# A two-layer hybrid transformer block on one core: elementwise steps moved off GpSimd, and modulation rows made in a layout of 128 channels a partition

## The chip, the core and the metric

The kernel runs on one core of one Trainium2 chip. The metric is the device time of one execution in microseconds. The core has five engines with instruction queues of their own: TensorE (PE in the profile; its weight loads PEld), VectorE (DVE), ScalarE (ACT), GpSimd (POOL) and SyncE (SP), which here issues nearly all DMAs. Each engine takes its instructions in the order written for it.

## What is computed

Two layers over 256 context and 256 latent tokens of 1024 channels. In each, three mixers run on projections of the modulated input (neighbourhood attention, RWKV-7, mLSTM); their outputs go through `w_out`, a residual sum and a layer norm, and then through a routed mixture of 32 experts (two per token) with a residual sum and a second norm. Cut to the lines that the change touches:

```python
for l in range(DEPTH):                                   # 2
    sh1, sc1, g1, sh2, sc2, g2 = split(silu(c) @ w_mod[l] + b_mod[l], 6)   # one row of 1024 each; other rows for ctx
    ...
    y_ctx, y_lat = token_mixers(p_ctx, p_lat, na_rpb[l], ...)
    x = layer_norm(alpha * x + g1 * dot(y_lat, w_out[l]), ln1_g[l], ln1_b[l])
    h2 = x * (1 + sc2) + sh2                             # the same for ctx in layer 0
    f = hierarchical_moe(h2, ...)
    x = layer_norm(alpha * x + g2 * f, ln2_g[l], ln2_b[l])

def neighbourhood_attention(...):    # s_loc = q.k * scale + bias from rpb, inside a window
def _rwkv_output(...):               # (head_norm(y) * ln_w + ln_b + bonus) * gate
```

All arithmetic is in f32 or its TensorE form (`fp32r`). In layer 1 only the latent tokens go past the mixers.

## The kernel before

Tokens lie on the 128 partitions in four tiles (0 and 1 context, 2 and 3 latents); layer 1 uses two of them behind the mixers. A layer runs through these stages, with the times of layer 0 / layer 1: projections and mixers (0 to 420 / 1085 to 1440 us), out stage (420 to 533 / 1440 to 1506), routing (533 to 548 / 1506 to 1520), expert blocks (548 to 1085 / 1520 to 2000), second norm.

A scheduler orders each engine's instructions from priorities and gives tiles their buffers. Work of one stage fills gaps of another: the projections of the attention and the mLSTM (`ps<-rg,wh` in the trace) lie between the steps of the RWKV inversion, and the `w_out` products (`pw<-rg,q`, `rg,yrw`, `rg,O`) between the attention's. In `moe` the order is the one that is written, and an expert weight ring of 1 MB pieces streams from DRAM once the routing has written the expert table.

The steps that the change touches:
- The RWKV chunk inversion (L754 and L756 on VectorE, 64 x n x n, growing n) and the T updates (L769), whose results TensorE takes up through ScalarE's copy L824. T then feeds the product PV x MA (`pw<-PV,MA`) and the ones behind it.
- `na_bias1` loads a bias table of 128 x 2048 (16 DMAs of 64 KB from `rpb`) and adds the window's mask to it, L1238 on GpSimd. There are two a layer. Attention takes them up much later.
- `headnorm` (L890) and `rwkv_out` (L906): mean, square (L899), variance, scale; transposes; sum with the bonus (L923).
- `out_rows` (L1378), called for tile 0 and tile 2: three modulation rows are broadcast from the DRAM tile `modd` to 128 partitions (512 KB each on the SBUF side), and four GpSimd instructions fold the first norm's scale and shift into them (L1383 to L1387).
- `out_item` (L1389), one a token tile: `w_out` product in two halves, residual (L1406, L1407), statistics (L1339, L1341), the routed input h (L1415, L1416, with the rows of `out_rows`), its transposes and logits, its split into an upper part `hi` (L1440, ScalarE) and a lower part `lo` (L1441, GpSimd), and the norm of the residual stream z, whose scale and shift are L1444 and L1445 on GpSimd.
- L1901, on GpSimd, scales the g2 rows by 1/ALPHA.

Of the kernel before, what the change touches and what calls it, by code (L numbers as in the profile page):

```python
# [9 lines left out]
F32 = mybir.dt.float32  # L10
# [4 lines left out]
AF = mybir.ActivationFunctionType  # L15
ALU = mybir.AluOpType
# [3 lines left out]
D = 1024  # L20
DEPTH = 2
# [5 lines left out]
ALPHA = (2.0 * DEPTH) ** 0.25  # L27
# [186 lines left out]
class K:  # L214
    def __init__(self, tc, ctx, a, dbg=None, upto=99):
        self.tc, self.nc, self.ctx, self.a = tc, tc.nc, ctx, a
        self.dbg = dbg or (lambda *x: None)
        self.upto = upto
        nc = self.nc
        self.cp = ctx.enter_context(tc.tile_pool(name="cp", bufs=1))  # L220
        self.ring = ctx.enter_context(tc.tile_pool(name="ring", bufs=NR))
        self.psp = ctx.enter_context(tc.tile_pool(name="psp", bufs=PB, space=PSUM))
        self.psw = ctx.enter_context(tc.tile_pool(name="psw", bufs=PC, space=PSUM))
        self.pse = ctx.enter_context(tc.tile_pool(name="pse", bufs=PE_, space=PSUM))
        if CFG["PD"]:
            self.psd = ctx.enter_context(tc.tile_pool(name="psd", bufs=CFG["PD"], space=PSUM))
        self.n = 0
        self.pin = False
        cp = self.cp
        self.cst = cp.tile([P, _CN], F32, name="cst")  # L230
        self.prm = cp.tile([P, DEPTH, _NP], F32, name="prm")
        self.ident = self.c("ident")
        self.one = cp.tile([P, 1], F32, name="one")
        nc.vector.memset(self.one, 1.0)
        self.epsc = cp.tile([P, 4], F32, name="epsc")
        for i, e in enumerate((LN_EPS, RW_EPS, ML_EPS, LN_EPS / ALPHA ** 2)):
            nc.vector.memset(self.epsc[:, i:i + 1], e)
        nc.scalar.preload_act_table_set("natural_log_exp_and_others")
        self.hp = ctx.enter_context(tc.tile_pool(name="hp", bufs=NH))
        self.wp = ctx.enter_context(tc.tile_pool(name="wp", bufs=NW))  # L240
        self.qp = ctx.enter_context(tc.tile_pool(name="qp", bufs=NQ))
        self.mp = ctx.enter_context(tc.tile_pool(name="mp", bufs=2))
        dp = ctx.enter_context(tc.tile_pool(name="dp", bufs=1, space=bass.MemoryType.DRAM))
        self.modd = [dp.tile([2, 6 * D], F32, name=f"modd{l}") for l in range(DEPTH)]
        self.xd = dp.tile([4 * P, D], F32, name="xd")
        self.nMd = dp.tile([8, 512], F32, name="nMd")
        self.eMd = dp.tile([8, 512], F32, name="eMd")
        self.dA, self.dX, self.dXT = ([dp.tile([16 * 4160], F32, name=f"{n}{i}") for i in range(4)] for n in ("dA", "dX", "dXT"))
        self.rst = cp.tile([P, 512], BF, name="rst")
        nc.gpsimd.memset(self.rst, 1.0)  # L250
        nc.gpsimd.memset(self.rst.rearrange("p (c s) -> p c s", s=64)[:, :, 0:1], 0.0)
# [638 lines left out]
    def headnorm(self, Y, n, eps, sq, s):  # L890

        nc = self.nc
        b = lambda t: t.unsqueeze(2).to_broadcast([P, n, 64])
        m = self.sm([16], s + "m", bufs=1)[:, :n]
        nc.vector.tensor_reduce(m, Y, AX.X, ALU.add)
        nc.vector.tensor_scalar(m, m, 1.0 / 64, None, ALU.mult)
        nc.vector.tensor_tensor(Y, Y, b(m), ALU.subtract)
        sq = sq[:, :n * 64].rearrange("p (n s) -> p n s", s=64)
        nc.gpsimd.tensor_tensor(sq, Y, Y, ALU.mult)  # L899
        v = self.sm([16], s + "v", bufs=1)[:, :n]  # L900
        nc.vector.tensor_reduce(v, sq, AX.X, ALU.add)
        nc.scalar.activation(v, v, AF.Ln, scale=1.0 / 64, bias=self.epsc[:, eps:eps + 1])
        nc.scalar.activation(v, v, AF.Exp, scale=-0.5)
        nc.vector.tensor_tensor(Y, Y, b(v), ALU.mult)

    def rwkv_out(self, last):  # L906
        nc = self.nc
        c0 = 4 if last else 0
        lo = c0 * 64
        self.headnorm(self.Ys[:, c0 * 128:].rearrange("p (n s) -> p n s", s=64), (8 - c0) * 2, 1, self.w("sq"), "rw")  # L910
        ys = self.Ys.rearrange("p (c x s) -> p c x s", x=2, s=64)
        self.yrw = self.w("yrw")
        for hh in range(2):
            pt = self.pw()
            for c in range(c0, 8):
                self.tr(pt[:, c * 64:(c + 1) * 64], ys[64 * hh:64 * hh + 64, c, :, :], 64 * hh)
            for ct in range(2):
                nc.scalar.activation(self.yrw[64 * hh:64 * hh + 64, ct * 512 + lo:(ct + 1) * 512], pt[64 * ct:64 * ct + 64, lo:], AF.Copy)
        for ct in range(2):
            sl = slice(ct * 512 + lo, (ct + 1) * 512)  # L920
            yo = self.yrw[:, sl]
            nc.vector.tensor_scalar(yo, yo, self.pr[:, 30 + ct:31 + ct], self.pr[:, 32 + ct:33 + ct], ALU.mult, ALU.add)
            nc.gpsimd.tensor_tensor(yo, yo, self.Vf[:, sl], ALU.add)  # L923
            pg = self.pw()
            self.mm(pg[:, lo:], self.g2w[0:64, ct * 128:(ct + 1) * 128], self.GD[0:64, lo:])
            nc.vector.tensor_tensor(yo, yo, pg[:, lo:], ALU.mult)
# [301 lines left out]
    def na_bias1(self, l, i):  # L1228

        nc = self.nc  # L1230
        rp = self.a["rpb"]
        b = self.rg((2048,))
        bv = b.rearrange("p (h r c) -> p h r c", h=8, r=4)
        for h in range(8):
            for a_ in range(2):
                off = ((l * 8 + h) * 15 + 7 - (2 * i + a_)) * 127
                nc.sync.dma_start(bv[64 * a_:64 * a_ + 64, h], bass.AP(tensor=rp.tensor, offset=off, ap=[[1, 64], [127, 4], [1, 64]]))
        nc.gpsimd.tensor_tensor(b.rearrange("p (n c) -> p n c", c=64), b.rearrange("p (n c) -> p n c", c=64),  # L1238
                                self.c("nam")[:, None, :].to_broadcast([P, 32, 64]), ALU.add)
        return b  # L1240

# [116 lines left out]
    def out_prep(self, l, last):  # L1358
        nc, a = self.nc, self.a
# [12 lines left out]
        nc.gpsimd.dma_start(self.rw, a["rtw"][l].rearrange("p (k n) -> p k n", k=KT))  # L1372
        self.rb = self.mp.tile([P, 40], F32, name=self.nm("rb"), tag="rb", bufs=1)
        nc.gpsimd.dma_start(self.rb, bass.AP(tensor=a["rtb"].tensor, offset=l * 40, ap=[[0, P], [1, 40]]))
        self.lnr = self.row(a["ln1_g"][l]), self.row(a["ln1_b"][l])
        self.Lg = self.mp.tile([P, 4, 40], F32, name=self.nm("Lg"), tag="Lg", bufs=1)

    def out_rows(self, l, i):  # L1378

        G = self.nc.gpsimd  # L1380
        lng, lnb = self.lnr
        g1, sh2, sc2 = self.rows3 = [self.row(self.modd[l][i, (2 + k) * D:(3 + k) * D]) for k in range(3)]
        G.tensor_scalar(sc2, sc2, 1.0, None, ALU.add)  # L1383
        tm = self.w("tm")
        G.tensor_tensor(tm, lnb, sc2, ALU.mult)
        G.tensor_tensor(sh2, sh2, tm, ALU.add)
        G.tensor_tensor(sc2, sc2, lng, ALU.mult)  # L1387

    def out_item(self, l, last, t):  # L1389

        nc, a = self.nc, self.a
        V, G = nc.vector, nc.gpsimd
        if t in (0, 2):
            self.out_rows(l, 1 - t // 2)
        g1, sh2, sc2 = self.rows3
        lng, lnb = self.lnr
        n = self.tl.index(t)
        z = self.acc[t]
        for hf in range(2):
            sl = slice(hf * 512, (hf + 1) * 512)  # L1400
            ps = self.pw()
            for k, kt in enumerate((4, 5, 6, 7, 0, 1, 2, 3)):
                yt, o = self.yn[kt]
                i = self.mm(ps, yt[:, o + t * 128:o + (t + 1) * 128], self.wo[kt // 2][:, kt % 2, sl], k == 0, k == 7)
            tm = self.q("tm")
# [5 lines left out]
        h2 = self.w("h2")  # L1411
        mean, rstd, nmr = self.stats(z, 0)
        for hf in range(2):
            sl = slice(hf * 512, (hf + 1) * 512)
# [17 lines left out]
        hi, lo = self.w("hi", F32R), self.w("lo", F32R)  # L1432
        self.hh_[t], self.hl_[t] = hi, lo
        pj = lambda x: x.rearrange("t (p j) -> t p j", j=KT)
# [3 lines left out]
                nc.scalar.activation(jp(hi), pj(h2), AF.Copy)  # L1438
        else:
            nc.scalar.activation(jp(hi), pj(h2), AF.Copy)  # L1440
        G.tensor_tensor(jp(lo), pj(h2), jp(hi), ALU.subtract)  # L1441
        if fin:
            self.norm_z(z, mean, rstd, nmr)
        G.tensor_tensor(z, z, lng, ALU.mult)  # L1444
        G.tensor_tensor(z, z, lnb, ALU.add)  # L1445

    def row(self, src):

# [274 lines left out]
    def moe(self, l):  # L1723
        nc = self.nc
# [50 lines left out]
        with self.tc.issue_after(self.slotted.ins):  # L1775
            for _ in self.more:
                pass
        nxt, gath = prep(*plan[1])
        run(up[4:], gath)
        for k in range(1, len(plan) + 1):  # L1780
# [73 lines left out]
    def run(self):  # L1854
# [15 lines left out]
        for l in range(DEPTH):  # L1870
# [26 lines left out]
            if self.upto == 10 * l + 2:  # L1897
                return
            for i in ((0,) if last else (1, 0)):
                self.g2b[i] = self.row(self.modd[l][i, 5 * D:6 * D])  # L1900
                nc.gpsimd.tensor_scalar(self.g2b[i], self.g2b[i], 1.0 / ALPHA, None, ALU.mult)  # L1901
            more = iter(())
            if l + 1 < DEPTH:
                more = self.mod_first(l + 1)
# [115 lines left out]
```

## Time and profile before

| | us |
|---|---|
| median of three runs | 2030.6 (2022.24 to 2033.0) |
| the profiled execution | 2033.04 |
| its span | 2031.2 |
| TensorE busy | 1800.4 (89%) |
| VectorE busy | 958.3 (47%) |
| ScalarE busy | 508.8 (25%) |
| GpSimd busy | 273.5 (13%) |

The profile is of one execution. An instruction's row gives its start, its duration, the engine, the line, the operation and the tiles. A bracket at its end tells how long the engine stood idle before it, and what released it. Wait rows sum such idle times. The granted clock is a share of TensorE's full speed: 1.00 is 2.4 GHz, 0.50 is 1.2 GHz.

### The profile page before, as it was taken

To read this page: it belongs to the slowest core of one execution; us is meant where nothing else is said; L and a number is where in the kernel's file an instruction comes from. 1 tells how busy PE (TensorE), PEld (TensorE's weight loads), DVE (VectorE), ACT (ScalarE), POOL (GpSimd) and SP (SyncE) were. 2 spreads that over 40 slices of the span, in tenths; PEclk is the share of its full clock that TensorE was granted. 3 is DMA by queue.
4 is the path that set the end of the run, shared out by engine and by line. 5 is a ranking of instruction groups with operands and counts; after the bars stand their busy time and mean duration, and the time that the engine had idled before them with its cause. 6 is when DMAs were issued, how large, how long until landed. Compare 5 with 4: busy or idle time off the path is not lost. (4 is left out here: it accounts for less than half of the span.)

```text
span 2031.2 us, 29550 instructions
## 1 busy us (share of the span) xinstructions
PE 1800.4 (89%) x11375; PEld 912.1 (45%) x11375; DVE 958.3 (47%) x2133; ACT 508.8 (25%) x1073; POOL 273.5 (13%) x204
## 2 busy tenths in 40 slices
PE   6999999799998899889996899997999988988884
PEld 2777875245533233324434677773453222323221
DVE  2686655567633334334446687744762222222223
ACT  1663413444110010001014654314521010100001
POOL 0000010034311112111221010010220001001001
PEclk9988999999999999999998899988899999999997
DMA  8432335733779998999992233347748979999995
GB/s 282 141 82 58 89 62 217 244 145 104 285 284 382 409 384 327 407 394 396 386 413 87 88 89 95 67 114 251 290 177 350 388 288 415 417 416 409 417 418 227
DMA packets 194224, 532.93 MB, mean 262 GB/s; under 512 B 77824, under 2 KB 108448, under 8 KB 156576
## 3 DMA queue, kind: packets, MB, share of 16 engines
q1 hardware_dynamic: 191936, 526.33, 68.9%
q0 software_dynamic: 992, 2.53, 0.4%
q8 instruction: 92, 1.51, 0.3%
q10 hardware_dynamic: 1152, 2.13, 0.3%
q14 instruction: 52, 0.43, 0.1%
HBM read 523.44 MB, written 7.50 MB: 261 GB/s over the span
## 5 line engine op out<-in xcount | busy, mean ns | idle before, releaser
L283 PE MATMUL ps<-rg,xe 128*32 128x512 f32 (+2 forms) x2280 | 478.0, 614 | 47.3 <-DMA rg<-in_exp_w_up_dram 27.7
L283 PE MATMUL pe<-rg,HT 128*32 128x512 f32 (+2 forms) x1120 | 236.0, 658 | 55.5 <-DMA rg<-in_exp_w_down_dram 44.4
L283 PE MATMUL ps<-rg,wh 128*128 128x512 f32 (+2 forms) x1056 | 260.0, 390 | 5.0 <-ACT wh L473 2.7
L283 PEld LDWEIGHTS ps<-rg,xe 128*32 128x32 f32 (+2 forms) x2280 | 107.8, 123 | 282.6 <-issue 180.3
L1686 DVE TENSOR_TENSOR sc<-pw,bc 128x512 f32<-128x512 f32 x164 | 112.1, 690 | 220.3 <-PE pw L283 218.9
L283 PEld LDWEIGHTS ps<-rg,wh 128*128 128x128 f32 (+1 forms) x1056 | 182.4, 195 | 53.8 <-issue 13.3
L1687 POOL TENSOR_TENSOR acc<-acc,sc 128x512 f32<-128x512 f32 x82 | 106.0, 1293 | 587.5 <-DVE sc L1686 587.5
L283 PEld LDWEIGHTS pe<-rg,HT 128*32 128x32 f32 (+2 forms) x1120 | 66.0, 131 | 220.6 <-issue 122.0
L1676 DVE SCALAR_TENSOR_TENSOR yl<-pe,sw,yh 128x512 fp32r<-128x512 f32 x54 | 40.4, 750 | 237.4 <-ACT yh L1675 234.6
L1675 ACT ACTIVATE yh<-pe,sw 128x512 fp32r<-128x512 f32 x54 | 36.9, 687 | 311.1 <-PE pe L283 288.2
L1652 ACT ACTIVATE H<-ps 128x512 f32<-128x512 f32 x27 | 16.1, 598 | 313.1 <-DVE acc L1687 302.9
L283 PE MATMUL pw<-oh,hi 128*128 128x256 f32 x336 | 90.7, 306 | 1.5 <-DVE oh L1590 1.5
L283 PE MATMUL pw<-yh,ot 128*128 128x512 f32 x164 | 84.2, 513 | 1.8 <-DVE sc L1686 1.5
L283 PE MATMUL pw<-oh,lo 128*128 128x256 f32 x336 | 83.8, 285 | 0.0
L283 PEld LDWEIGHTS pw<-yh,ot 128*128 128x128 f32 x164 | 30.7, 187 | 116.4 <-DVE sc L1686 57.6
L283 PEld LDWEIGHTS pw<-oh,hi 128*128 128x128 f32 x336 | 64.7, 192 | 39.8 <-issue 24.1
L283 PE MATMUL ps<-wh,rg 128*128 128x256 f32 x384 | 77.7, 294 | 0.0
L1622 POOL TENSOR_TENSOR ot<-m,m 128x512 fp32r<-128x512 f32 (+1 forms) x27 | 27.3, 1011 | 328.7 <-PE pw L287 282.5
L1624 DVE SCALAR_TENSOR_TENSOR m<-m,row 128x512 f32<-128x512 f32 (+1 forms) x54 | 28.3, 561 | 91.3 <-POOL ot L1622 91.3
L283 PE MATMUL pw<-yl,ot 128*128 128x512 f32 x164 | 65.7, 400 | 0.7 <-DVE yl L1676 0.5
L1687 DVE TENSOR_TENSOR acc<-acc,sc 128x512 f32<-128x512 f32 x82 | 64.6, 787 | 2.6
L283 PEld LDWEIGHTS pw<-oh,lo 128*128 128x128 f32 x336 | 65.0, 193 | 1.0 <-issue 1.0
(418 smaller groups left out, 2619.9 us busy)
## 6 DMA issues: line engine op xcount, KB each, us to landing
rg<-in_exp_w_up_dram SPq DMA_DIRECT2D x127, 1024.0 KB, 11.2
rg<-in_exp_w_gate_dram SPq DMA_DIRECT2D x126, 1024.0 KB, 10.4
rg<-in_exp_w_down_dram SPq DMA_DIRECT2D x124, 1024.0 KB, 10.6
rg<-in_w_mod_dram SPq DMA_DIRECT2D x40, 1024.0 KB, 7.0
rg<-in_w_in_dram SPq DMA_DIRECT2D x26, 1024.0 KB, 5.5
rg<-in_w_mod_dram SPq DMA_DIRECT2D x16, 512.0 KB, 9.5
rg<-in_w_out_dram SPq DMA_DIRECT2D x8, 1024.0 KB, 8.7
bc<-modd SPq DMA_DIRECT2D x12, 512.0 KB, 5.2
```

The costliest lines, as they stand in the source:

```text
L283: return self.inorder(self.nc.tensor.matmul(out, lhsT, rhs, start=start, stop=stop, skip_group_check=True))
L1622: nc.gpsimd.tensor_tensor(ot, m[0], m[1], ALU.add)
L1624: V.scalar_tensor_tensor(m[k], m[k], 1.0, self.wrow[k][:, :T], ALU.mult, ALU.mult, accum_out=sw[:, k:k + 1])
L1652: nc.scalar.activation(H, pgu[0][b], AF.Silu)
L1675: nc.scalar.activation(yh[:, sl], py[h2], AF.Copy, scale=sw)
L1676: V.scalar_tensor_tensor(yl[:, sl], py[h2], sw, yh[:, sl], ALU.mult, ALU.subtract)
L1686: V.tensor_tensor(tm, ps, self.g2b[0 if t >= 2 else 1][:, sl], ALU.mult)
L1687: (V if hf else nc.gpsimd).tensor_tensor(self.acc[t][:, sl], self.acc[t][:, sl], tm, ALU.add)
```

## The change

- `rows_prep`, new and called at the start of the out stage, makes the modulation rows once a layer for both token kinds, in tiles of 16 partitions x 128 channels (8 partitions a token kind): ten small loads, five VectorE instructions (L1398 to L1402), three stores into a new DRAM tile `rowd`. `out_rows` then broadcasts g1 from `modd` and the two finished rows from `rowd`. The g2 rows come from `rowd` too, and L1901 is gone.
- The mask add goes from GpSimd to VectorE (L1239 in the changed file).
- The lower part `lo` goes from GpSimd to VectorE (L1458).
- In the RWKV output, the sum goes from GpSimd to VectorE (L924), the square of the head norm from GpSimd to ScalarE (L900).
- The scale and shift of the first norm leave `out_item`. They are done on VectorE in `moe`, behind the instruction that writes the slot table (L1795): 8 instructions of 128 x 1024 in layer 0, 4 in layer 1.

```diff
@@ __init__
+        self.rowd = [dp.tile([3, 2 * D], F32, name=f"rowd{l}") for l in range(DEPTH)]
@@ headnorm
-        nc.gpsimd.tensor_tensor(sq, Y, Y, ALU.mult)
+        nc.scalar.activation(sq, Y, AF.Square)
@@ rwkv_out
-            nc.gpsimd.tensor_tensor(yo, yo, self.Vf[:, sl], ALU.add)
+            nc.vector.tensor_tensor(yo, yo, self.Vf[:, sl], ALU.add)
@@ na_bias1
-        nc.gpsimd.tensor_tensor(b.rearrange("p (n c) -> p n c", c=64), b.rearrange("p (n c) -> p n c", c=64),
+        nc.vector.tensor_tensor(b.rearrange("p (n c) -> p n c", c=64), b.rearrange("p (n c) -> p n c", c=64),
                                 self.c("nam")[:, None, :].to_broadcast([P, 32, 64]), ALU.add)
@@ out_prep
+        self.rows_prep(l)
         self.lnr = self.row(a["ln1_g"][l]), self.row(a["ln1_b"][l])
@@ out_rows
-        G = self.nc.gpsimd
-        lng, lnb = self.lnr
-        g1, sh2, sc2 = self.rows3 = [self.row(self.modd[l][i, (2 + k) * D:(3 + k) * D]) for k in range(3)]
-        G.tensor_scalar(sc2, sc2, 1.0, None, ALU.add)
-        tm = self.w("tm")
-        G.tensor_tensor(tm, lnb, sc2, ALU.mult)
-        G.tensor_tensor(sh2, sh2, tm, ALU.add)
-        G.tensor_tensor(sc2, sc2, lng, ALU.mult)
+        self.rows3 = [self.row(self.modd[l][i, 2 * D:3 * D])] + [self.row(self.rowd[l][k, i * D:(i + 1) * D]) for k in range(2)]
+
+    def rows_prep(self, l):
+        nc = self.nc
+        V = nc.vector
+        md, rd = self.modd[l], self.rowd[l]
+        t = self.q("rp")[:16].rearrange("p (k s) -> p k s", k=4)
+        g = self.sm([128], "rg2", bufs=1)[:16]
+        at = lambda src, i, k: bass.AP(tensor=src.tensor, offset=src.offset + i * 6 * D + k * D, ap=[[128, 8], [1, 128]])
+        for i in range(2):
+            r = slice(8 * i, 8 * i + 8)
+            nc.sync.dma_start(t[r, 0], at(md, i, 3))
+            nc.sync.dma_start(t[r, 1], at(md, i, 4))
+            nc.sync.dma_start(t[r, 2], at(self.a["ln1_g"][l], 0, 0))
+            nc.sync.dma_start(t[r, 3], at(self.a["ln1_b"][l], 0, 0))
+            nc.sync.dma_start(g[r], at(md, i, 5))
+        V.tensor_scalar(t[:, 1], t[:, 1], 1.0, None, ALU.add)
+        V.tensor_tensor(t[:, 3], t[:, 3], t[:, 1], ALU.mult)
+        V.tensor_tensor(t[:, 0], t[:, 0], t[:, 3], ALU.add)
+        V.tensor_tensor(t[:, 1], t[:, 1], t[:, 2], ALU.mult)
+        V.tensor_scalar(g, g, 1.0 / ALPHA, None, ALU.mult)
+        for k, x in ((0, t[:, 0]), (1, t[:, 1]), (2, g)):
+            nc.sync.dma_start(rd[k].rearrange("(p s) -> p s", s=128), x)
@@ out_item
-        G.tensor_tensor(jp(lo), pj(h2), jp(hi), ALU.subtract)
+        V.tensor_tensor(jp(lo), pj(h2), jp(hi), ALU.subtract)
         if fin:
             self.norm_z(z, mean, rstd, nmr)
-        G.tensor_tensor(z, z, lng, ALU.mult)
-        G.tensor_tensor(z, z, lnb, ALU.add)
@@ moe
         with self.tc.issue_after(self.slotted.ins):
             for _ in self.more:
                 pass
+            for t in self.tl:
+                for x, op in zip(self.lnr, (ALU.mult, ALU.add)):
+                    V.tensor_tensor(self.acc[t], self.acc[t], x, op)
@@ layer
-                self.g2b[i] = self.row(self.modd[l][i, 5 * D:6 * D])
-                nc.gpsimd.tensor_scalar(self.g2b[i], self.g2b[i], 1.0 / ALPHA, None, ALU.mult)
+                self.g2b[i] = self.row(self.rowd[l][2, i * D:(i + 1) * D])
```

The scheduler's order moves with it. Three places in the program follow; line numbers of the changed file are one or more higher.

VectorE in the RWKV inversion of layer 0, before (`inv` is the matrix being inverted, `T` the blocks put together from it, `wh` an input of a projection, `PV` a factor of the product):

```order
L754 TENSOR_TENSOR inv_1818<-inv_1818 64x6x6
L474 TENSOR_TENSOR wh_2938<-rg_2878,wh_2938 128x512
L756 TENSOR_REDUCE inv_1818<-inv_1818 64x6
L754 TENSOR_TENSOR inv_1818<-inv_1818 64x7x7
L756 TENSOR_REDUCE inv_1818<-inv_1818 64x7
L754 TENSOR_TENSOR inv_1818<-inv_1818 64x8x8
L769 TENSOR_TENSOR T_1225<-pw_1796,T_1225 128x4x64
L756 TENSOR_REDUCE inv_1818<-inv_1818 64x8
L769 TENSOR_TENSOR T_1225<-pw_1797,T_1225 128x4x64
```

and of the changed kernel:

```order
L755 TENSOR_TENSOR inv_1820<-inv_1820 64x6x6
L475 TENSOR_TENSOR wh_2940<-rg_2880,wh_2940 128x512
L757 TENSOR_REDUCE inv_1820<-inv_1820 64x6
L1239 TENSOR_TENSOR rg_3087<-rg_3087,cst 128x2048
L755 TENSOR_TENSOR inv_1820<-inv_1820 64x7x7
L770 TENSOR_TENSOR T_1227<-pw_1798,T_1227 128x4x64
L757 TENSOR_REDUCE inv_1820<-inv_1820 64x7
L770 TENSOR_TENSOR T_1227<-pw_1799,T_1227 128x4x64
```

The mask add (L1239, `rg_3087`) now stands between two inversion steps, ahead of both T updates (L770).

TensorE at the same place, before: projection matmuls (`rg,wh`), and then the product that waits for T:

```order
L283 MATMUL ps_2880<-rg_210,wh_2870 128x512 x2
L283 MATMUL ps_2880<-rg_211,wh_2870 128x512
L283 MATMUL ps_2880<-rg_210,wh_2870 128x512
L283 MATMUL ps_2880<-rg_357,wh_2873 128x512
L283 MATMUL pw_1860<-PV_650,MA_1247 64x64
L283 MATMUL pw_1860<-PV_650,MA_1248 64x64
```

and of the changed kernel:

```order
L284 MATMUL ps_2882<-rg_212,wh_2872 128x512 x2
L284 MATMUL ps_2882<-rg_213,wh_2872 128x512
L284 MATMUL ps_2882<-rg_212,wh_2872 128x512
L284 MATMUL ps_2882<-rg_359,wh_2875 128x512
L284 MATMUL ps_2882<-rg_360,wh_2875 128x512
L284 MATMUL ps_2882<-rg_359,wh_2875 128x512 x2
L284 MATMUL ps_2882<-rg_360,wh_2875 128x512
L284 MATMUL ps_2882<-rg_359,wh_2875 128x512 x2
L284 MATMUL ps_2882<-rg_360,wh_2875 128x512
L284 MATMUL pw_1862<-PV_652,MA_1249 64x64
L284 MATMUL pw_1862<-PV_652,MA_1250 64x64
```

Twelve projection matmuls (an x2 row is two) stand ahead of the product, where there were five.

SP in the out stage of layer 0, where `rp` and `rg_3733` are the 16-partition tiles, `bc` the broadcast rows, and the L323 loads prefetch the next layer's `w_mod`:

```order
L1395 DMA rp_3732<-in_ln_g_dram 8x128
L1396 DMA rp_3732<-in_ln_b_dram 8x128
L1404 DMA rowd_97<-rg_3733 16x128
L323 DMA rg_4548<-in_w_mod_dram 128x2048
L1404 DMA rowd_97<-rp_3732 16x128 x2
L1465 DMA bc_3881<-rowd_97 128x1024
L1465 DMA bc_3883<-rowd_97 128x1024
L1465 DMA bc_4361<-modd_94 128x1024
L323 DMA rg_4554<-in_w_mod_dram 128x2048
```

VectorE at the first out tile of the changed kernel, up to the use of these rows:

```order
L1424 SCALAR_TENSOR_TENSOR acc_3712<-acc_3712,tm_3894 128x512
L1400 TENSOR_TENSOR rp_3732<-rp_3732 16x128
L1340 BN_STATS bst_3910<-acc_3712 128x6
L1401 TENSOR_TENSOR rp_3732<-rp_3732 16x128
L1423 TENSOR_TENSOR tm_3906<-pw_3897,bc_3879 128x512
L1424 SCALAR_TENSOR_TENSOR acc_3712<-acc_3712,tm_3906 128x512
L1340 BN_STATS bst_3910<-acc_3712 128x6
L1342 BN_AGGR bmv_3913<-bst_3910 128x2
L1356 SCALAR_TENSOR_TENSOR brs_3915<-bmv_3913,brs_3915 128x1
L1432 SCALAR_TENSOR_TENSOR h_3909<-acc_3712,bmv_3913,bc_3883 128x512 x2
```

The row loads (`bc_3881`, `bc_3883`) stand behind stores that wait for L1401, and h (L1432) takes `bc_3883` up; before, the loads read `modd` and GpSimd worked on the rows in between.

TensorE behind the `w_out` product of that tile, before: `w_out` matmuls of a later tile (`yrw`, `O` and `q` are the mixers' outputs), and then the transposes of h:

```order
L287 MATMUL ps_3912<-cst,pg_3823 128x128 x2
L283 MATMUL pw_4104<-rg_3718,yrw_2140 128x512 x2
L283 MATMUL pw_4104<-rg_3720,O_2181 128x512 x2
L283 MATMUL pw_4104<-rg_3722,q_2583 128x512
L287 MATMUL pe_3944<-cst,h_3892 128x128 x4
```

and of the changed kernel:

```order
L284 MATMUL pw_3897<-rg_3726,q_2836 128x512 x2
L284 MATMUL pw_4119<-rg_3720,yrw_2142 128x512 x2
L284 MATMUL pw_4119<-rg_3722,O_2183 128x512 x2
L284 MATMUL pw_4119<-rg_3724,q_2585 128x512 x2
L284 MATMUL pw_4119<-rg_3726,q_2836 128x512
L284 MATMUL pw_4131<-rg_3720,yrw_2142 128x512 x2
L288 MATMUL pe_3961<-cst,h_3909 128x128 x4
```

Nine matmuls of later tiles stand ahead of the transposes, where there were five.

## Rows read from the trace of the kernel before

**Rows 1.** Busy time by stage: window, us, TensorE, weight loads, VectorE, ScalarE, GpSimd, clock, DMA share, GB/s.

```profile
420.00:533.00 113.00, 105.82 (x521) 55.12 (x519) 77.83 (x152) 45.99 (x103) 51.65 (x21) 0.98 0.36 126
...
590.00:1085.00 495.00, 446.75 (x2377) 166.18 (x2376) 200.89 (x353) 41.62 (x66) 89.20 (x69) 0.98 0.95 380
```

**Rows 2.** TensorE's waits, 250 to 600 us: us in total, times, longest.

```profile
PE pw L283 <- ACT T L824: 4.3, 1, 4.3
```

**Rows 3.** TensorE's waits, 1300 to 1560 us.

```profile
PE pw L287 <- DVE Ys L904: 3.7, 1, 3.7
...
PE ps L283 <- DVE Es L1501: 0.9, 1, 0.9
```

**Rows 4.** GpSimd's instructions by line and form: busy us, mean ns, idle before.

```profile
L1238 POOL TENSOR_TENSOR rg<-rg,cst 128x2048 f32<-128x2048 f32 x4 | 18.2, 4558 | 238.9 <-DMA rg<-in_rpb_dram 147.1 <-DVE inv L756 91.8
...
L1441 POOL TENSOR_TENSOR lo<-h,hi 128x1024 fp32r<-128x1024 f32 x6 | 17.5, 2913 | 12.1 <-ACT hi L1440 12.1
```

**Rows 5.** VectorE's timeline in the two inversions: start, us, instruction.

```profile
269.88 0.19 DVE L754 TENSOR_TENSOR inv<-inv 64x25 f32<-64x25 f32 x1
...
271.09 4.47 DVE L754 TENSOR_TENSOR inv<-inv 64x36 f32<-64x36 f32 x1
...
1319.43 4.59 DVE L754 TENSOR_TENSOR inv<-inv 64x81 f32<-64x81 f32 x1
```

**Rows 6.** TensorE's timeline at the same places.

```profile
272.23 1.43 PE L283 MATMUL ps<-rg,wh 128*128 128x512 f32 x5
277.96 3.47 PE L283 MATMUL pw<-PV,MA 128*64 128x64 f32 x60 [4.30 <-ACT T L824]
...
1325.56 2.62 PE L283 MATMUL pw<-PV,MA 128*64 128x64 f32 x44 [4.33 <-ACT T L824]
```

**Rows 7.** TensorE by window: us, busy, granted clock, DMA share, GB/s.

```profile
278.00:283.00 5.00, 5.00 (x70) 0.50 0.22 42
...
1325.60:1330.00 4.40, 4.40 (x51) 0.50 0.01 4
1330.00:1335.00 5.00, 5.00 (x18) 0.52 0.20 24
```

**Rows 8.** VectorE's sums by line: ns min/median/max, first and last start, forms.

```profile
L996 DVE TENSOR_TENSOR wl<-rg,wh x12: 1195/1220/1228, 139.6 to 1341.8; 128x1024 fp32r<-128x1024 f32 x12
...
L474 DVE TENSOR_TENSOR wh<-rg,wh x88: 414/684/1217, 28.6 to 1306.3; 128x512 fp32r<-128x512 f32 x84, 128x256 fp32r<-128x256 f32 x4
```

**Rows 9.** VectorE's timeline at the RWKV output of layer 0.

```profile
328.92 1.22 DVE L901 TENSOR_REDUCE rwv<-sq 128x16 f32<-128x1024 f32 x1 [0.92 <-POOL sq L899]
```

**Rows 10.** VectorE's and TensorE's timelines at layer 0's first out tile.

```profile
433.47 0.69 DVE L1339 BATCH_NORM_STATS2 bst<-acc 128x6 f32<-128x512 f32 x1
...
441.44 1.41 DVE L1415 SCALAR_TENSOR_TENSOR h<-acc,bmv,bc 128x512 f32<-128x512 f32 x2 [1.26 <-POOL bc L1387]
...
436.54 1.88 PE L283 MATMUL pw<-rg,yrw 128*128 128x512 f32 x4
...
443.57 1.78 PE L287 MATMUL pe<-cst,h 128*128 128x128 f32 x8 [2.57 <-DVE h L1416]
```

**Rows 11.** DMA issues: queue, count, KB each, median us to landing.

```profile
rg<-in_exp_w_up_dram SPq DMA_DIRECT2D x127, 1024.0 KB, 11.2
...
bc<-modd SPq DMA_DIRECT2D x12, 512.0 KB, 5.2
...
dX<-inv SPq DMA_DIRECT2D x8, 64.0 KB, 2.5
```

**Rows 12.** VectorE's timeline in the routing of layer 1.

```profile
1506.94 2.30 DVE L1478 TENSOR_TENSOR rt<-Lg,rt 128x8 f32<-128x8 f32 x1
```

**Rows 13.** VectorE's and TensorE's timelines, first expert block of layer 0.

```profile
556.33 0.69 DVE L1608 COPY xe<-pw 128x512 f32<-128x512 f32 x1 [2.81 <-PE pw L283]
563.87 0.27 DVE L372 COPY modT<-ps 128x16 f32<-128x16 f32 x2 [6.85 <-PE ps L287]
...
563.67 2.74 PE L283 MATMUL ps<-wx,xe 128*128 128x512 f32 x6
```

## The prediction

> **What bounds the kernel now.** I read the busy time by stage first. In the out stage of layer 0 TensorE is busy 105.82 of 113 us and VectorE 77.83; in the expert blocks the DMA engines are busy 0.95 of the time at 380 GB/s [rows 1]. So there are two kinds of stretch. From a layer's start to its routing, TensorE sets the pace and idles only where another engine is late. Behind the routing, the weight stream does, and it starts when the routing's table is there: a microsecond saved ahead of it is one saved at the end, while work put on VectorE inside it can hide.
>
> Second, the waits of TensorE ahead of the expert blocks. The largest single one is 4.3 us for ACT's T [rows 2]; layer 1 has the same one, 4.33 us, in the timeline [rows 6]. Layer 1 has another of 3.7 us for the rwkv head norm [rows 3].
>
> Third, what ends the T wait. VectorE's small inversion step L754 takes 0.19 us at 269.88, but 4.47 us at 271.09 and 4.59 us at 1319.43 [rows 5]. Those are the times in which GpSimd runs its mask add L1238, whose mean is 4558 ns [rows 4]: a VectorE instruction with two SBUF operands sits until the GpSimd one ends, and the two T updates (L769) stand behind it in VectorE's queue. The GpSimd work that the change moves does its harm here, by holding VectorE, and not by its own lateness.
>
> Fourth, the granted clock. After the wait in layer 0 it is 0.50 in 278 to 283; after that of layer 1, 0.50 and 0.52 in 1325.6 to 1335 [rows 7]. That is the 1.2 GHz level, on streaming matmuls.
>
> **Part A, the mask add on VectorE (L1238).** It removes the hold and puts the add itself in the queue, one small step later than the held L754. VectorE's 128x1024 sum takes 1.22 us and its 128x512 one 0.684 [rows 8], so 128x2048 is estimated at 1.22 + 2 x 0.54 = 2.30 us. The T updates come earlier by 4.47 - 0.19 - 2.30 = 2.0 us in layer 0, and as much in layer 1. TensorE's order changes too: in layer 0 it gets 7 more matmuls of the next projection ahead of PV x MA, in layer 1 nine. One costs 1.43 / 5 = 0.286 us [rows 6], so 2.0 and 2.6 us of work now lie in the wait. Of the 4.30 us, 0.3 are left; of the 4.33, nothing. That the work pulled ahead is missed at a later wait can't be excluded: the gain is 2.0 if all of it is missed and 4.0 if none, 2.0 to 4.3 in layer 1. Next, the clock. Five us at 0.50 lose 2.5 us, and 4.4 us at 0.50 with 5 at 0.52 lose 4.6 [rows 7]. With no long wait ahead of them these come back wholly, or not at all if the rest of the low activity there is enough to halve the clock. So layer 0 gives 2.0 to 6.5 and layer 1 2.0 to 8.9, A together 4.0 to 15.4. I take the middle of each part: 3 + 3.2 for the waits and 3.5 for the clock, about 10. The second add of each layer stands where VectorE isn't waited for; if its 2.30 us do stand ahead of a product that TensorE needs, they cost up to that much once. I take 0.3.
>
> **Part B, the rwkv output.** The square L899 goes from GpSimd to ScalarE, the sum L923 to VectorE. In layer 0 VectorE waited 0.92 us for the square [rows 9]. In layer 1 TensorE waits 3.7 us for the normalised Ys [rows 3], a chain in which the square is one link of several. The gain is 0 (ScalarE as slow, chain ends elsewhere) to 0.92 a layer; I take 1 for both.
>
> **Part C, the modulation rows.** Four GpSimd passes over 128x1024 a row set become five VectorE instructions on 16 partitions x 128, each like the 0.19 us one [rows 5], so about 1 us a layer. To this come ten small loads, three stores and the row loads, which now read the new DRAM tile. For the first out tile of layer 0 the path is this: L1401 stands behind that tile's first statistics, which end at 433.47 + 0.69 = 434.2 [rows 10]; plus 0.2; store 2.5 us (nearest row, 64 KB); row load 5.2 us (the same rows from another source) [rows 11]: landed at 442.1. Before, VectorE took up the rows at 441.44, after a wait for GpSimd of 1.26 us [rows 10]. So the rows come 0.7 us later, not earlier. But TensorE now has four more out projection matmuls ahead of the transposes of h; two take 1.88 us (four records) [rows 10], so the four are 3.76 us of work. They cover the 2.57 us wait and the 0.7: gain 2.57. If the store and the load meet a loaded queue, as the weight loads that take 11.2 us [rows 11], 6.0 us more than the 5.2, the rows come 6.7 us later and the four matmuls cover 3.76 - 2.57 = 1.2 of it: a loss of 5.5. The second row set's loads wait for tile 1's h alone and are far ahead of tile 2; I take nothing for it. On SP the stores wait for VectorE with two prefetches of w_mod behind them, which are needed much later: no cost. C gives -5.5 to 2.6, taken 2.5.
>
> The Trainium skill, page "DMA: Bandwidth & Descriptors", section "Anatomy of one DMA — SWDGE (gpsimd) path" (these go by SP's queue), puts some 2.0 us on every transfer, mostly the receipt of the last write, and the bytes over 436 GB/s on top. By it a trip through DRAM is never free: a store and a row load in series would be an estimated 2.0 + 3.2 = 5.2 us. The rows say 7.7. With the page's price the rows would land at 439.6, ahead of VectorE's need; C would be the same 2.5, since the four matmuls cover either, and the slower rival below would lose half its chance. I keep the rows.
>
> **Part D, lower parts and the norm's affine step.** L1441 (2913 ns on GpSimd [rows 4]) moves to VectorE, at 1.22 us if its strided read costs nothing, and I bound it by GpSimd's time above. Six of them are 7.3 to 17.5 us of VectorE time in stages where VectorE has 113 - 78 = 35 us free in layer 0 alone [rows 1], and GpSimd's holds go with them. In layer 1's routing the hold is on the chain: L1478, a 128x8 step, took 2.30 us at 1506.94 [rows 12]. But L1441 now stands right behind it, and TensorE waited only 0.9 us there [rows 3], for the rest it was busy. Gain: 0.9 at most, a loss of up to 1 if L1441 is slow; I take 0.3. The affine step becomes 8 VectorE instructions in layer 0 (4 in layer 1) behind the routing, 8 x 1.22 = 9.8 us. Three stand ahead of the copy at 556.33, 3.7 us where VectorE was idle for 2.81 [rows 13], so the copy comes 0.9 us late; it makes the second half of a block's tokens, whose matmuls TensorE takes up at 563.67 [rows 13], behind those of the first half, and that hides it. The other five, 6.1 us, lie between the copy and 563.9, where VectorE had nothing to do. Without this cover the first expert block would be 0.9 us late; with another 1.22, if one more slips ahead, 2.1.
>
> **Sum.** 10 - 0.3 + 1 + 2.5 + 0.3 = 13.5 us. Against the profiled execution's 2033.0 us (span 2031.2 and 1.8 around it) that is 2019.5. The median of the runs shown is 2.4 us below the profiled one, so I predict 2017.1. All low ends together give 4.0 - 2.3 + 0 - 5.5 - 1 - 2.1 = -6.9, all high ends 15.4 + 1.8 + 2.6 + 0.9 = 20.7, that is 2037.5 and 2009.9.
>
> **Rivals.**
> 1. *The cut stalls refill.* The matmuls pulled ahead are missed later and the clock halves anyway. For it: VectorE's chain gains 2.0 us a layer, and no more; nothing else sets TensorE's pace in the inversions. Against it: TensorE has other projections to fill with. A gives 4.0, the sum 7.5: 2025.5, less 2.4 is 2023.1.
> 2. *The add waits for its table.* GpSimd could wait for the bias table's DMA with nobody behind it; on VectorE every inversion step and T update is queued behind. Before, GpSimd took the table up when VectorE's step of 271.09 was held, so it had landed by about then; VectorE now reaches the add some 1 us after that. From 3 us of lateness on, A's waits are back where they were: the sum is 3.5, that is 2027.1.
> 3. *The hold isn't GpSimd's doing.* Then the change moves work, and L754 stays slow: A gives 0 and VectorE has more to do; the sum is 3, that is 2027.6. The match of 4.47 with the GpSimd instruction's time, twice, speaks against it.
> 4. *The rows come late: slower.* Each row set now hangs on three transfers in series behind one VectorE instruction. If each takes the loaded 11.2 us in place of 2.5 to 5.2 [rows 11], a set comes about 3 x 7 = 21 us later; the first set of layer 0 and the only one of layer 1 stand on the path, with about 1 us of cover in the first and a few in the second, so 35 us, of which 11 are given back by the rest: 2030.6 + 24 = 2054.6. It decides from 11 us lost on, so from some 8 us of lateness a set. Against it: the DMA engines are not full in the out stages, which the 5.2 us of the row loads already reflects.
>
> **How the numbers follow.** What a measurement of this kernel can tell from no change is about 0.5%, 10 us. Forecast (gain of 10 to 21 against the median, 2009.9 to 2020.4): 0.60. Rival 1: 0.22. Rival 2: 0.05. Rival 3: 0.07. Rival 4: 0.06. Faster by over 0.5% (under 2020.4) is the forecast and a little of rival 1: 0.62. Slower: rival 4, 0.06. The rest, 0.32, is within. The range leaves out rival 4 and what lies past rival 3; below, it goes 3 us under the high ends, since other holds in the out stage are not priced singly: 2007 to 2029.
>
> **What would show it.** Right: in the changed profile no L754 over 0.5 us; the add on VectorE near 2.3 us; T waits under 1 us; the clock near 1.00 behind them; h of the first out tile not waited for. Wrong: L1239 taking longer than 3 us or idle time ahead of it for the bias table's DMA (rival 2); a granted clock of 0.5 in the same places (rival 1); VectorE idle for the new rows ahead of L1432 for more than 2 us (rival 4); the first expert copy in layer 0 waiting behind the affine step.

## The result, and the profile after

| | us |
|---|---|
| before, median of six runs | 2028.01 (2022.24 to 2033.0) |
| changed, median of six runs | 2013.99 (2004.66 to 2020.73) |
| ratio, 95% interval | 0.9925 (0.9905 to 0.9944) |
| span of the profiled execution, before / changed | 2031.2 / 2002.9 |

The change saves 0.75%, some 15 us (11 to 19 by the interval). The profiled execution of the changed kernel is the quickest of its six, at a mean granted clock of 0.962 against 0.949 in that of before; so the spans stand 28 us apart where the medians stand 14, and amounts are taken from the ratios and not from the spans.

The engines, from the page of the changed kernel:

```profile
PE 1780.3 (89%) x11375; PEld 900.6 (45%) x11375; DVE 961.9 (48%) x2169; ACT 509.6 (25%) x1075; POOL 163.6 (8%) x161
```

GpSimd lost 110 us of work. VectorE now does the mask, the lower parts and the affine step (9.2, 11.6 and 14.6 us by the rows below), with the sums of the RWKV output and the small rows some 40 us, and is busy for only 3.6 us more than before. The instructions that both kernels have take 32 us less, added up: a VectorE instruction that is held (it has begun, and stands until GpSimd's is done) counts as busy for all that time. The two long inversion steps make 8.6 of the 32 us. Nearly as much, 8.0, is in the attention, where VectorE scales the probabilities `pg` (its 128 x 512 form, all instructions of the kernel before and then of the changed one: busy us, mean ns, idle before):

```profile
L1275 DVE TENSOR_SCALAR pg<-pg,smx 128x512 f32<-128x512 f32 x32 | 23.2, 726 | 0.1
...
L1276 DVE TENSOR_SCALAR pg<-pg,smx 128x512 f32<-128x512 f32 x32 | 15.2, 475 | 0.1
```

VectorE's timeline of the changed kernel in the inversion of layer 0, and then of layer 1, answers to [rows 5]:

```profile
268.42 0.20 DVE L755 TENSOR_TENSOR inv<-inv 64x36 f32<-64x36 f32 x1
...
269.25 2.27 DVE L1239 TENSOR_TENSOR rg<-rg,cst 128x2048 f32<-128x2048 f32 x1
...
271.71 0.42 DVE L770 TENSOR_TENSOR T<-pw,T 128x256 f32<-128x256 f32 x1
...
1313.79 2.29 DVE L1239 TENSOR_TENSOR rg<-rg,cst 128x2048 f32<-128x2048 f32 x1
1316.00 0.31 DVE L755 TENSOR_TENSOR inv<-inv 64x100 f32<-64x100 f32 x1
```

The step that took 4.47 us takes 0.20, and the add takes 2.27. TensorE at the same places, against [rows 6]:

```profile
269.56 3.01 PE L284 MATMUL ps<-rg,wh 128*128 128x512 f32 x12
272.60 1.97 PE L284 MATMUL pw<-PV,MA 128*64 128x64 f32 x60
...
1317.24 1.50 PE L284 MATMUL pw<-PV,MA 128*64 128x64 f32 x44 [0.22 <-ACT T L825]
```

No wait is left in layer 0, 0.22 us in layer 1, and the product itself takes 1.97 us in place of 3.47. Its clock, by window, against [rows 7] (us, busy, granted clock, DMA share, GB/s):

```profile
274.00:279.00 5.00, 5.00 (x64) 1.00 0.50 83
...
1319.00:1324.00 5.00, 5.00 (x32) 1.00 0.37 52
```

TensorE's waits in layer 0, 245 to 600 us, and then in layer 1, 1280 to 1550 us (from the second `Wp` row on), against [rows 2, 3]. `Wp` and `O` are tiles of the mLSTM, `pg` the attention's probabilities, `Ys` the RWKV output:

```profile
PE ps L284 <- DVE Wp L1131: 11.0, 5, 4.3
PE ps L288 <- DVE pg L1276: 3.0, 2, 1.5
...
PE pw L284 <- DVE O L1189: 2.0, 1, 2.0
...
PE ps L284 <- DVE pg L1284: 0.8, 1, 0.8
PE pw L288 <- DVE Ys L905: 0.8, 1, 0.8
...
PE ps L284 <- DVE Wp L1131: 3.2, 2, 2.7
PE pw L288 <- DVE Ys L905: 3.2, 1, 3.2
...
PE pw L284 <- ACT T L825: 0.2, 1, 0.2
```

Those of the out stage of layer 0 in the kernel before (420 to 545 us) were these:

```profile
PE pe L287 <- DVE h L1416: 2.6, 1, 2.6
PE ps L283 <- DVE pg L1283: 2.3, 2, 1.6
PE ps L287 <- DVE pg L1275: 1.2, 1, 1.2
...
PE pw L283 <- DVE O L1188: 0.2, 1, 0.2
```

The wait for h is gone, and most of one for pg; O and the other pg have taken it over: 6.3 us before, 3.0 + 2.0 + 0.8 = 5.8 after (the 0.8 stands at 417.55, in a stage that begins earlier now). In layer 1 two rows of the kernel before, from 1300 to 1560 us, belong beside those above:

```profile
PE ps L283 <- DMA rg<-in_w_mod_dram: 5.0, 4, 1.7
...
PE ps L283 <- DVE Wp L1130: 0.6, 1, 0.6
```

So the waits for Wp grow by 2.6 us in each layer (8.4 before in layer 0), and the 5.0 us of waits for loads of `w_mod` are gone.

The first out tile of the changed kernel, VectorE, SP's queue with its waits from 425 to 450 us, and TensorE, against [rows 10]:

```profile
436.63 0.26 DVE L1401 TENSOR_TENSOR rp<-rp 16x128 f32<-16x128 f32 x1
...
443.37 1.41 DVE L1432 SCALAR_TENSOR_TENSOR h<-acc,bmv,bc 128x512 f32<-128x512 f32 x2 [1.52 <-DMA bc<-rowd]
...
436.12 1.10 SPq L1404 DMA_DIRECT2D rowd<-rp  x2
437.47 1.14 SPq L1465 DMA_DIRECT2D bc<-rowd  x2
...
SPq L1465 <- DMA rowd<-rp: 0.7, 2, 0.4
...
444.52 1.88 PE L284 MATMUL pw<-rg,yrw 128*128 128x512 f32 x4
446.23 1.04 PE L288 MATMUL pe<-cst,h 128*128 128x128 f32 x8
```

VectorE waits 1.52 us for the new rows, where it waited 1.26 for GpSimd; TensorE doesn't wait, since the added `w_out` matmuls run until the transposes begin.

The moved instructions on VectorE (ns min/median/max, first and last start):

```profile
L1239 DVE TENSOR_TENSOR rg<-rg,cst x4: 2272/2288/2293, 269.2 to 1329.8; 128x2048 f32<-128x2048 f32 x4
...
L1458 DVE TENSOR_TENSOR lo<-h,hi x6: 1909/1938/1990, 451.7 to 1483.7; 128x1024 fp32r<-128x1024 f32 x6
...
L1795 DVE TENSOR_TENSOR acc<-acc,bc x12: 1215/1217/1224, 547.8 to 1503.3; 128x1024 f32<-128x1024 f32 x12
```

The routing of layer 1 on VectorE, against [rows 12], and the first expert copy of layer 0 with TensorE's use of it, against [rows 13]:

```profile
1483.65 0.15 DVE L1493 TENSOR_TENSOR rt<-Lg,rt 128x8 f32<-128x8 f32 x1
1483.72 1.91 DVE L1458 TENSOR_TENSOR lo<-h,hi 128x1024 fp32r<-128x1024 f32 x1
...
551.21 0.68 DVE L1623 COPY xe<-pw 128x512 f32<-128x512 f32 x1
...
557.39 3.60 PE L284 MATMUL ps<-wx,xe 128*128 128x512 f32 x8
```

### The profile page after: what moved, and what is told of

Read it like the earlier page. It is cut to its first block, busy times and chain, and to the rows that moved or that the text cites. A ratio compares the mean times of both kernels' runs of the same rounds, so it can differ in the third digit from the quotient of the medians.

```text
span 2002.9 us, 29551 instructions
## 1 busy us (share of the span) xinstructions
PE 1780.3 (89%) x11375; PEld 900.6 (45%) x11375; DVE 961.9 (48%) x2169; ACT 509.6 (25%) x1075; POOL 163.6 (8%) x161
## 5 line engine op out<-in xcount | busy, mean ns | idle before, releaser
L284 PE MATMUL ps<-rg,wh 128*128 128x512 f32 (+2 forms) x1056 | 255.5, 386 | 4.5 <-ACT wh L474 2.7
L1621 ACT ACTIVATE xe<-pw 128x512 f32<-128x512 f32 x28 | 16.7, 597 | 183.6 <-PE pw L284 183.6
```

The source lines that it names most:

```text
L284: return self.inorder(self.nc.tensor.matmul(out, lhsT, rhs, start=start, stop=stop, skip_group_check=True))
L1621: nc.scalar.activation(x[:, j2 * 2:j2 * 2 + 2, :n], ps[:, :, :n], AF.Copy)
```

## The experiments

Each was timed against the kernel before on the same chip. Ratios are to before, with the 95% interval.

**The mask add alone**, on VectorE, all else as before.

```diff
-        nc.gpsimd.tensor_tensor(b.rearrange(...), b.rearrange(...), mask, ALU.add)
+        nc.vector.tensor_tensor(b.rearrange(...), b.rearrange(...), mask, ALU.add)
```

> The kernel before with one edit: the mask add of the bias tables on VectorE. Theory (the hold of VectorE by GpSimd's add is most of the gain): no inversion step over 0.6 us, TensorE's waits for T of 4.3 us under 0.5 us in both layers, the granted clock behind them back near 1.00, and the time about 10 us below before, 0.995 of it. Rival (the matmuls pulled ahead are missed later): the T waits go, but others of about 2 us appear behind them and the time falls by 4 us, 0.998. Second rival (the out stage's freed GpSimd is what paid): no more than 2 us, 0.999 or above.

Measured: 0.9945 (0.9926 to 0.9963), 11 us. TensorE at the product in both layers, and its waits in layer 1:

```profile
271.50 1.97 PE L283 MATMUL pw<-PV,MA 128*64 128x64 f32 x60
...
1314.34 1.50 PE L283 MATMUL pw<-PV,MA 128*64 128x64 f32 x44 [0.22 <-ACT T L824]
...
PE ps L283 <- DVE Es L1501: 2.3, 1, 2.3
```

Both T waits are gone, as in the changed kernel. The wait for Es (the experts chosen for a token) in the routing of layer 1, 0.9 us before [rows 3], is 2.3 here: there L1441 and L1445 are still on GpSimd, and a little of the gain goes back.

**All but the mask add**: the changed kernel with that line on GpSimd.

> The changed kernel with the mask add back on GpSimd, all else as changed. Theory: the two T waits of 4.3 us and the slow clock behind them are back, the time is about 10 us above the changed kernel, so some 4 us below before (0.998). Rival (refill): 4 us above the changed kernel, 10 below before (0.995). Second rival (out stage): within 2 us of the changed kernel (0.993).

Measured: 0.9974 (0.996 to 0.9988), 5 us below before, on the chip of the run above.

```profile
273.55 3.47 PE L284 MATMUL pw<-PV,MA 128*64 128x64 f32 x60 [4.13 <-ACT T L825]
...
1318.70 2.35 PE L284 MATMUL pw<-PV,MA 128*64 128x64 f32 x44 [3.90 <-ACT T L825]
```

Both waits are back, and 5 to 10 us with them (0.9974 against 0.9925, and against 0.9947 when the changed kernel was measured again, below; the second pair of intervals overlaps). One edit alone and all others without it agree on its direction and, as far as these intervals tell, on its size.

**The mask add in eight pieces on GpSimd**, in the kernel before. The orders of VectorE and TensorE are those of before, row by row.

```diff
+        for s in range(8):
+            x = b[:, s * 256:(s + 1) * 256].rearrange("p (n c) -> p n c", c=64)
+            nc.gpsimd.tensor_tensor(x, x, mask of 4 x 64, ALU.add)
```

> The kernel before with GpSimd's mask add cut into eight of 128x256 (about 0.6 us each); the order of VectorE and TensorE is that of before, row by row. Theory (a VectorE instruction with two SBUF operands sits until the running GpSimd instruction ends): no inversion step over 0.8 us, several of 0.3 to 0.7 in their place, T waits of 4.3 us down to about 2 (no matmuls are pulled ahead here), time 3 to 6 us below before (0.998). Rival (the small step is slow because of its operands or its DMA, not of GpSimd): one step of 4 us stays and the time is that of before. Second rival (the two engines share by turns, so a step waits for as many pieces as come): the T waits stay at 4 us though no single step is long.

Measured: 0.9952 (0.9932 to 0.9972), 10 us: as much as the move to VectorE. VectorE's inversion steps, two of GpSimd's pieces, and TensorE at the product:

```profile
L754 DVE TENSOR_TENSOR inv<-inv x120: 142/254/843, 124.3 to 1316.9; 64x1 f32<-64x1 f32 x8, 64x4 f32<-64x4 f32 x8, 64x9 f32<-64x9 f32 x8, 64x16 f32<-64x16 f32 x8
...
274.67 0.73 POOL L1240 TENSOR_TENSOR rg<-rg,cst 128x256 f32<-128x256 f32 x1 [7.42 <-DVE T L862]
276.27 0.94 POOL L1240 TENSOR_TENSOR rg<-rg,cst 128x256 f32<-128x256 f32 x1 [0.88 <-DMA rg<-in_rpb_dram]
...
269.86 1.97 PE L283 MATMUL pw<-PV,MA 128*64 128x64 f32 x60
...
1313.07 1.50 PE L283 MATMUL pw<-PV,MA 128*64 128x64 f32 x44 [0.23 <-ACT T L824]
```

No step is longer than 0.84 us. This run decides two things. The hold is GpSimd's doing, and it ends with the GpSimd instruction: the add, its engine and its operands are those of before, only its length is not. And the gain needs neither VectorE's faster add nor the matmuls pulled ahead. It also does more than cut: a piece waits for its own two loads only, so the pieces lie spread out (24 of the 32 stood behind a DMA of the table), and few meet the steps before T. I had expected half the wait to stay.

**The changed kernel with these pieces.**

> The changed kernel, with the mask add on GpSimd again but in eight pieces of 128x256. Theory (only the length of the GpSimd instruction did harm): no inversion step over 0.9 us, no T wait over 0.5 us, and the time of the changed kernel within 2 us, 0.993 of before; VectorE has 9.2 us less to do, which may give back up to 3 us where TensorE waits for Wp (11.0 us in the changed kernel, 8.4 in the one with pieces alone). Rival (VectorE's speed at the add is what paid): the T waits are back in part and the time is 4 us or more above the changed kernel, 0.9955.

Measured: 0.9942 (0.992 to 0.9963). TensorE's waits in layer 0, VectorE's steps, and one step beside one piece:

```profile
PE ps L284 <- DVE Wp L1131: 8.4, 5, 3.2
...
L755 DVE TENSOR_TENSOR inv<-inv x120: 142/276/881, 119.2 to 1316.3; 64x1 f32<-64x1 f32 x8, 64x4 f32<-64x4 f32 x8, 64x9 f32<-64x9 f32 x8, 64x16 f32<-64x16 f32 x8
...
264.44 0.74 POOL L1241 TENSOR_TENSOR rg<-rg,cst 128x256 f32<-128x256 f32 x1 [0.44 <-DMA rg<-in_rpb_dram]
...
264.48 0.73 DVE L755 TENSOR_TENSOR inv<-inv 64x16 f32<-64x16 f32 x1
```

The step of 64 x 16 that begins behind the start of a piece takes 0.73 us, as long as the piece; in the changed kernel the same step takes 0.16 (at 266.14). VectorE's order is row by row that of the run with all but the mask add, so the two differ by the cut alone: the T waits of 4.13 and 3.90 us there are none in layer 0 and 0.6 in layer 1 here (I had allowed 0.5). The time can't be told from the changed kernel's. The 2.6 us of waits for Wp that the changed kernel has more in layer 0 are gone, and nothing that can be measured is won by it.

**Each mask add twice on VectorE** (a second, like instruction behind the first).

> The changed kernel with each mask add made twice on VectorE (the window's values stay, the masked ones are twice as low): four more instructions of 2.3 us, one of them in each inversion with the mask, behind the T updates. Theory (the add is covered by projection matmuls): within 3 us of the changed kernel, 0.993 to 0.995. Rival (VectorE is near the bound in the inversions, and what the add costs there is on the path): 2.3 us for each of the four and the slower clock again, so 9 us or more above, 0.9975.

Measured: 0.992 (0.9898 to 0.9943), the changed kernel's time, with 9.2 us more on VectorE.

**No mask add.**

> The changed kernel without the mask add (the neighbourhood window is not masked, so this part of the computation is left out). Theory (the add is covered): the time of the changed kernel within 2 us, 0.992 to 0.9935. Rival (the add's 2.3 us are on VectorE's path to T and Wp): 4 to 9 us below the changed kernel, 0.990.

Measured: 0.9919 (0.9893 to 0.9945), the same again. With none, one or two adds of 2.3 us, the time stays, within the some 5 us that these intervals resolve. The waits do move: in layer 0 the one for Ys is 0.8 us with one add and 4.9 with two. What showed in the time was the long hold ahead of the T updates.

**The out stage alone**: rows, lower parts and affine step as changed, the mask add and both RWKV edits as before.

> The changed kernel with the mask add and both RWKV output edits back where they were: rows through DRAM, lower parts on VectorE, affine step behind the routing alone. Theory: 2.5 us from the rows and 0.3 from the rest, so 3 us below before (0.9985); the wait for h of the first out tile of layer 0 (2.57 us) is gone. Rival (out stage): 8 to 12 us below before (0.995). Second rival (the rows come late): above before by 3 us or more (1.0015).

Measured: 0.9977 (0.996 to 0.9994), 5 us. From the run with all but the mask add it differs by the RWKV edits alone, by 0.0003: their worth, forecast at 1 us, is below what these runs resolve.

**The rows alone**: `rows_prep` and `out_rows` as changed, all else as before.

> The kernel before with one edit: the modulation rows in the small layout and through DRAM (with the g2 rows); mask, lower parts, sums and affine step stay on GpSimd. Theory as predicted: the 2.57 us wait for h of the first out tile goes and nothing else, so 2.5 us below before, 0.9988. Rival (from the changed kernel with these rows made on GpSimd, which stood some 6 us above it): four long GpSimd passes a row set also hold VectorE in the attention beside them, so 5 to 6 us below before, 0.9973, with the waits for pg of 2.3 us gone too. Second rival (the rows come late): above before.

Measured: 0.9984 (0.9967 to 1.0001), 3 us, and none is within the interval. TensorE's waits in the out stage of layer 0:

```profile
PE ps L288 <- DVE pg L1276: 2.8, 2, 1.6
PE pw L284 <- DVE O L1189: 2.0, 1, 2.0
```

h is not waited for, and pg and O are, as in the changed kernel: the waits of this stage move with the rows edit. The stretch from the mLSTM's norm (the first `pe<-sq,cst` of the stage) to the routing's `ps<-rt,pcol` tells what is left of the 2.57 us. In layer 0 it takes 124.6 to 124.9 us in the three kernels with the old rows and the out stage's other steps on GpSimd (before, the mask add alone, the pieces), and 124.3 here (415.44 to 539.77); in layer 1 it is 73.0 to 74.1 and 72.3. So, by one execution of each, 0.3 to 0.6 us came where 2.5 was forecast, and 0.7 to 1.8 where nothing was. Holds went too: the 128 x 512 form of L1275 takes 17.8 us in all here, and 23.2 before.

**The rows on GpSimd in passes of 128 x 1024**, in the changed kernel.

> The changed kernel with the modulation rows made on GpSimd as before, in 128 x 1024 passes; all other edits stay. Theory: the wait of VectorE for GpSimd ahead of the first out tile's h is back and costs 2.5 us, so 0.994 of before. Rival (the path through DRAM is no quicker): the same time as the changed kernel or 1 to 3 us less, 0.992. Second rival (GpSimd's four passes hold VectorE elsewhere in the out stage): 6 us or more above the changed kernel, 0.9955.

Measured: 0.9956 (0.9938 to 0.9975), above the changed kernel's 0.9925 by 6 us and above the 0.9947 of its second measurement, below, by 2, on intervals that overlap: not resolved. TensorE's waits in layer 0:

```profile
PE pe L288 <- DVE h L1417: 2.9, 1, 2.9
PE ps L284 <- DVE pg L1284: 2.8, 1, 2.8
```

The wait for h is back, and a longer one for pg; the wait for O is gone (0.2). The 128 x 512 form of L1275 takes 19.8 us in all, and 15.2 in the changed kernel.

**The small row instructions on GpSimd**, in the 16 x 128 layout.

```diff
-        V.tensor_scalar(t[:, 1], t[:, 1], 1.0, None, ALU.add)
+        nc.gpsimd.tensor_scalar(t[:, 1], t[:, 1], 1.0, None, ALU.add)      # and the other four
```

> The changed kernel with the five small row instructions on GpSimd in place of VectorE, in the same 16 x 128 layout and through the same DRAM tile. Theory (what pays in this part is the small layout, which takes 128x1024 passes off GpSimd and off the path, and not the engine): the time of the changed kernel within 3 us, 0.993 of before. Rival (it is VectorE that pays): 4 us or more above the changed kernel, 0.995.

Measured: 0.9923 (0.9903 to 0.9944), the changed kernel's time. Which engine does these five instructions makes no difference that can be measured.

**Lower parts and affine step on GpSimd**, in the changed kernel.

> The changed kernel with the lower parts and the first norm's affine step back on GpSimd, where they were; rows, mask and RWKV edits stay. Theory: these two are worth 0.3 us and lie off the path, so the time is that of the changed kernel within 2 us (0.993 of before). Rival (GpSimd's holds in the out stage and in the routing cost): 4 to 6 us above the changed kernel (0.9955). Second rival (they burden VectorE): 2 to 4 us below the changed kernel (0.991).

Measured: 0.9939 (0.9916 to 0.9963): not told from the changed kernel. The 128 x 512 form of L1275 takes 17.8 us in all here too.

**The changed kernel once more**, beside the last two and the one with pieces.

> The changed kernel itself, once more, beside the three others on one chip. Theory: 0.9925 of before, 15 us, as measured. Rival (the first measurement was helped by the granted clock, which differs from run to run): 0.995 or more.

Measured: 0.9947 (0.9924 to 0.9969). The two measurements put the gain at 15 and 11 us, the intervals together at 6 to 19. Between my two forecasts for this run, 0.9925 and 0.995 or more, it does not decide.

## Why the prediction was right

The forecast was 2017.1 with a gain of 13.5 us; measured were 2014.0 and, by the ratios, 15 and 11 us. The cause of most of it, GpSimd's mask add holding VectorE ahead of T, was the one named. That the sum came so close is in part luck, since terms were off both ways.

**The mask add.** Forecast 10, measured 11 alone and 5 to 10 by undoing it. The two waits (8.6 us) and the slow clock went as the steps said. VectorE's price was 2.29 us for an estimate of 2.30, and it reached the add of each inversion with its table there (rival 2 didn't happen). Rival 1 gave this part 4 us, outside the interval of the mask add alone (7 to 15). No inversion step is longer than 0.54 us; the sign asked for 0.5, but the largest form takes 0.54 with nothing beside it. Two points were off, though. The matmuls pulled ahead were named as half of the cover; with the order of before and pieces on GpSimd the wait goes as well. And both terms were taken at their middle, 6.2 us for the waits and 3.5 for the clock, where both came out at their high end: 8.4 us of waits are gone, and the granted clock is 1.00 in the windows shown, worth the 7.1 us. That makes 15 us, of which 4 to 5 are missing in the time: the middle fitted by luck. Where they went stays open. Waits for Wp are 2.6 us longer in each layer of the changed kernel, and the one for Es 1.4 us longer with the mask add alone; but the waits for loads of `w_mod` in layer 1, 5.0 us before, are 0.8 with the mask add alone and 3.1 with the pieces, at the same time. The waits of a profile do not add up to the time here.

**Rival 3** is refuted by the pieces: the hold is GpSimd's. The Trainium skill, page "SBUF — State Buffer", section "SBUF: two separate sides", describes the port pair that VectorE and GpSimd share as an exclusive lock for the whole instruction. The pieces agree: with instructions of 0.73 us the longest step is 0.84 us, where it was 4.59, and the step shown beside a piece takes the piece's time.

**The rows.** Forecast 2.5, measured 3 with none in the interval. The wait for h went as the four matmuls said it would. But the sum took it as won, and it mostly wasn't: in the same stage O is waited for 1.8 us more, and pg, its two lines together, 0.3 us more (3.8 for 3.5), and the stretch from the mLSTM's norm to the routing is 0.3 to 0.6 us shorter in layer 0. So this step was wrong in its mechanism, and that 3 stands near 2.5 says nothing for it. It isn't refill in the sense of rival 1 either: O is waited for at 428.13, ahead of the four matmuls and not behind them, and VectorE's L1188 ahead of O had itself waited 1.42 us for ScalarE. The orders moved with the edit, which the prediction left out, and so did the holds of the attention beside the rows, some 5 us of VectorE's time on L1275 alone (23.2 to 17.8). What the edit is worth in the time, and by which of these, is not shown. The transfer was mis-sized too. From the end of L1401 (436.89) to the start of L1432 (443.37) it took 6.5 us and not 7.7. SP's wait row says that each row load did stand until its store had landed; but a store took 1.35 us (436.12 to 437.47 for the first) and not 2.5, and the second load, issued at 438.27, took 5.1 for an estimate of 5.2. The page "DMA: Bandwidth & Descriptors" of the Trainium skill, section "Anatomy of one DMA — SWDGE (gpsimd) path", would have 5.2 us in all by the estimate given in the prediction, 2.0 for the store and 3.2 for the load. The measured sum lies between, and neither term of the page's estimate fits these transfers on SP's queue.

**The rest.** The RWKV edits: the wait for Ys fell from 3.7 to 3.2 us in layer 1 [rows 3], within the bound of 0.92 and too small to measure in the time. L1441 on VectorE costs 1.94 us, inside 1.22 to 2.91; the step held for 2.30 us in the routing takes 0.15, and the wait for Es of layer 1 is gone. The affine step takes 1.217 us an instruction; the copy behind the first three ends at 551.89, and TensorE takes its half up at 557.39. **Rival 4** (slower) had no part: VectorE waited 1.52 us for the first rows, TensorE not at all.

## What to carry to other kernels

A long elementwise instruction on GpSimd cost time here where VectorE ran a chain of short ones beside it and TensorE waited for the end of that chain: look for one small VectorE instruction whose time equals that of a GpSimd one. Compare the time of the same instruction in two kernels, too, since a held VectorE counts as busy. Cutting the GpSimd instruction, along the borders of the loads that it waits for, was worth as much as moving it. A wait removed from an engine with in-order work is not yet time won: add up the waits of the whole stage before and after.

## What the runs showed of the hardware that I had not expected

That eight pieces on the slower engine give the whole gain: 0.9952 against 0.9945 for the move. That 9.2 us more work on VectorE, of which a rival had said that it stands on the path, cost nothing that can be measured (0.992 against 0.9925 and 0.9947). And that a sum of holds nearly as large as that of the two long steps lies in the attention, which the prediction did not price: L1275 takes 23.2 us before, 17.8 with the rows off GpSimd and the lower parts and the affine step on it, 19.8 the other way round, and 15.2 with both off.
